# Dropping an empty lane step before the first use of rows that were fetched ahead, and slowing the first lane's pace

## The chip, the cores and the metric

The kernel runs on one core of one Trainium2 chip. The metric is the device time of one execution in microseconds. "The profile" is one execution recorded by the hardware profiler; its views group instructions by engine: PE (TensorE matmuls; PEld are its weight loads), DVE (VectorE), ACT (ScalarE), POOL (GpSimd) and SP (SyncE, which issues nearly all DMAs here). L206 is line 206 of the kernel before.

## The reference

One layer of a hybrid encoder over 1280 rows (a sample of 1024, a prompt of 256) of width 2048. After an RMSNorm one large projection gives the inputs of three groups: a bidirectional state-space scan (SSD), windowed grouped-query attention, and cross-attention to a memory of 256 rows. Their gated outputs are concatenated and projected back.

```python
hn = rms_norm(x, norm_g)
proj = hn @ w_in
xbc, z_ssd, dt_raw, q, k, v, z_att, mq, z_mem = split_cols(proj, IN_SIZES)
...                                        # conv, SSD forward and backward, gate, norm -> o_ssd
q = rms_norm(q.reshape(b, T, ATT_HEADS, ATT_HEAD_DIM), q_norm_g)
k = rms_norm(k.reshape(b, T, ATT_KV_HEADS, ATT_HEAD_DIM), k_norm_g)
o_att = window_attention(q, k, v, sink) * jax.nn.silu(z_att)
...
mq = rms_norm(mq.reshape(b, T, MEM_HEADS, MEM_HEAD_DIM), mq_norm_g)
sm = jnp.einsum('bthd,bmhd->bhtm', mq, mk) * (MEM_HEAD_DIM ** -0.5)
o_mem = jnp.einsum('bhtm,bmhd->bthd', jax.nn.softmax(sm, axis=-1), mv) * jax.nn.silu(z_mem)
return x + jnp.concatenate([o_ssd, o_att, o_mem], axis=-1) @ w_out
```

## The kernel before

**Blocks.** The rows are ten tiles of 128, in two groups of five: tiles 0 to 4 and 5 to 9. The projections run as blocks of weights. A block of 512 columns for five tiles (`block_tok`) takes 16 weight slices, k = 0 to 15, with 15 matmuls each; a feature block (`block_feat`, x0 to x5, za, zm) has 16 k of 12 matmuls. Every float32 weight slice is loaded by SP, copied on ACT into a high part (L206) and its remainder formed on DVE (L207), so that three fast matmuls stand for one exact one. There are three buffers of high and low parts (`WB`) and four raw ones (`RB`). Blocks in order: the memory's two, q of the first group, fourteen units for the first group that save products by sums (`block_pair`), kv and z1 of the first group; then for the second group x0 to x5, kv, q, za0, za1, z0, z1, mq, zm0, zm1; the output blocks o0 to o3 of the first group; and eight `block_pair` units for the output of the second.

**Lanes.** All other work is written as Python generators, one per tile, that are queued on two lanes. One lane step runs a generator from one `yield` to the next and so puts that work between block matmuls. After each k, `run` calls `pump(rates)`: each lane is owed `rates[i]` more steps, and the two take turns while either is owed at least one. A step's instructions are tied behind the weight split of that k. The last call of a generator, after its last `yield`, is a step too. `RATES` gives the pace of either lane, by group and block; feature blocks use half of it per k. `need(fn, ts)` steps a lane at once until the named tiles are done: for the keys and attention before kv of the second group, and for the outputs before they are loaded as rows for the output blocks.

- The first lane holds: small vectors, the memory's keys (`mk_prep`) and values, then `k_prep` (norm, split and transpose of the keys of a tile), `attn` (window attention) and `mem_attn` (memory attention), in the order k_prep 0-4, attn 0-3, mem_attn 0-4, k_prep 5-9, attn 4, attn 5-9, mem_attn 5-7, the second memory's keys and values, mem_attn 8-9.
- The second lane holds the scan: `dt_prep`, `ssd_up` (forward) and `ssd_down` (backward).

**Rows fetched ahead.** `k_prep`, `attn` and `mem_attn` begin with rows that an earlier block stored to DRAM. Near its end each of them calls `fetch_next()`, which issues the load for the tile behind it in the lane, if that tile is one of these three and queued by then (`fetched`). The tile itself takes the loaded rows in `taken(...)`, or issues the load there if it was not fetched. Then came a `yield` in every case, and in the next step the first use: a square on ACT (L517 in k_prep, L632 in attn, L749 in mem_attn), a sum on DVE and a power on POOL. In mem_attn of the first group, PE's transpose of the rows (`turned`, L744) comes before the square; in the second group it is a step later. L757 and L759 split the turned rows in mem_attn.

**What is behind it.** In attn: five steps on, the transposes on PE (`pq`, L653); later four scores (`psc`, L671, L672, with the clamp and maximum `nm` on DVE, L673), four times turning the weights (`ppt`, L693, copied by L694 on ACT to `pT`), and two products with the values (`po`, L703). In k_prep three steps on: the transposes (`pk`, L536) of `kh` (L528, L530). In mem_attn: scores `pms` (L772 to L774), softmax `mpr`, turns `pmt` (L794), products `pmo` (L809). Of the second lane the text names `so` (L1040, ACT's copy of the turned result), `pyb` (L1091, the backward scan's product with the state) and `pd` (L1074, transposes).

Of the kernel before, what the change touches and what calls it, by code (L numbers as in the profile page):

```python
# [28 lines left out]
CH, WB, RB, WA, WBB = 4, 3, 4, 5, 4  # L29
RBB = 4  # L30

RATES = ({'kv': (4.0, 1.0), 'z1': (2.2, 1.7)},
         {'kv': (1.5, 1.5), 'x': (2.1, 2.15), 'q': (2.25, 2.5), 'za': (2.15, 2.5), 'z0': (2.1, 2.5),
          'z1': (2.1, 2.55), 'mq': (2.0, 2.7), 'zm': (1.75, 2.75), 'o': (2.15, 2.4)})
FAR = 1e30

UNITS = (0, 8, 1, 9, 2, 10, 3, 11, 4, 12, 5, 13, 6, 7)
# [7 lines left out]
def hymba_encoder_kernel(  # L45
# [37 lines left out]
    def psum(name):  # L83
        return mix.tile([P, 512], F32, tag="mix", name=name)
# [37 lines left out]
    def rsqrt(dst, src, scale, n):  # L122
        G.tensor_scalar(out=dst, in0=src, scalar1=scale, scalar2=EPS, op0=ALU.mult, op1=ALU.add)
        G.tensor_tensor(out=dst, in0=dst, in1=mhalf[:, :n], op=ALU.pow)

    def hv(ap, n=8):
        return ap.rearrange("p (h d) -> p h d", h=n)

    def hb(ap, n, d):
        return ap.unsqueeze(2).broadcast_to([P, n, d])  # L130
# [7 lines left out]
    def queue(lane, fn, ts):  # L138
        for t in ts:
            lanes[lane].append(((fn.__name__, t), fn(t)))  # L140
# [28 lines left out]
    def need(fn, ts):  # L169

        for t in ts:
            while (fn.__name__, t) not in done:
                step(next(x for x in lanes if any(nm == (fn.__name__, t) for nm, _ in x)))
# [47 lines left out]
    def w_in_rows(name):  # L221
        return w_laid(laid_in(name), W_AT[name][1])
# [107 lines left out]
    def ev_dtkv(base):  # L330
        def f(i, ps):
            t = base + i
            r = ev.tile([P, P], F32, tag="evt" if i % 2 else "evu", name="kraw")
            A.activation(r, ps[:, 32:160], AF.Copy)
            S.dma_start(k_d[t], r)
            V.tensor_add(dt_all[:, t, :], ps[:, :32], dtb)
            V.tensor_copy(v_all[:, i + (2 if base else 0), :], ps[:, 160:288])  # L337
        return f
# [4 lines left out]
    def some_left():  # L343
        with ExitStack() as st:
            for ins in marks:
                st.enter_context(tc.issue_after(ins))
            left.popleft()()
# [67 lines left out]
    def w2(name):  # L415
        return mp.tile([P, 512], F32, tag="wa", name=name, bufs=WA)
# [64 lines left out]
    fetched = {}  # L481
# [21 lines left out]
    def taken(name, t):  # L503
        return fetched.pop((name, t)) if (name, t) in fetched else fetch[name](t)

    def fetch_next():

        name = lanes[0][1][0] if len(lanes[0]) > 1 else ("", 0)
        if name[0] in fetch:
            fetched[name] = fetch[name[0]](name[1])  # L510

    def k_prep(t):
        r = taken("k_prep", t)
        yield
        ss = sm.tile([P, 2], F32, tag="s2", name="kss", bufs=4)
        sq = w2("ksq")[:, :P]
        A.activation(sq, r, AF.Square)  # L517
        V.reduce_sum(out=ss, in_=hv(sq, 2), axis=AX.X)
        rr = sm.tile([P, 2], F32, tag="s2", name="krr", bufs=4)
        rsqrt(rr, ss, 1.0 / 64, 2)  # L520
        yield
        r3 = hv(r, 2)
        V.tensor_mul(r3, r3, hb(rr, 2, 64))
        V.tensor_mul(r3, r3, gq.unsqueeze(1).broadcast_to([P, 2, 64]))

        kh = mp.tile([P, 4, 2, 64], F32R, tag="wa", name="kh", bufs=WA)
        for d in range(2):
            A.activation(kh[:, 0:2, d, :], r3, AF.Copy)  # L528
        for d in range(2):
            V.tensor_sub(kh[:, 2:4, d, :], r3, kh[:, 0:2, 0, :].bitcast(F32))  # L530
        yield
        yield
        ps = psum("pk")
        kf = kh.rearrange("p a b d -> p (a b d)")
        for a in range(4):
            T.transpose(ps[:, a * P:(a + 1) * P].bitcast(F32R), kf[:, a * P:(a + 1) * P], identr)  # L536
        sl = t if t < 5 else t - 3
        c = slice(sl * P, (sl + 1) * P)
        V.tensor_copy(kT[:, :, c], hv(ps[:, :256], 2))
        A.activation(kL[:, :, c], hv(ps[:, 256:], 2), AF.Copy)  # L540
        fetch_next()
        yield
# [77 lines left out]
    def attn(t):  # L620
# [5 lines left out]
        s0 = k0 if t < 4 else k0 - 3  # L626
        grp, ti = divmod(t, 5)
        tc_ = slice(ti * P, (ti + 1) * P)
        q = taken("attn", t)
        yield  # L630
        sq = w2("sq")
        A.activation(sq, q, AF.Square)  # L632
        ss = sm.tile([P, 8], F32, tag="s8", name="qss", bufs=4)
# [10 lines left out]
        for b in range(2):  # L644
# [9 lines left out]
            o = mp.tile([P, 512], F32R, tag="qT", name="qT", bufs=2)  # L654
# [79 lines left out]
    def mem_attn(t):  # L734
        grp, ti = divmod(t, 5)
        tc_ = slice(ti * P, (ti + 1) * P)
        qr = taken("mem_attn", t)
        q = qr.bitcast(F32)
        yield

        def turned():
            ps = psum("pmq")
# [689 lines left out]
    def run(gen, rates, after=None, hold=0, lag=2, extra=None):  # L1432

        for k in gen:
            if after is not None:
                pend.extend(after(k))
            if hold:
                for _ in range(2 if k < KT - 4 else 0):
                    if pend:
                        u = pend.popleft()()  # L1440
                        next(u)
                        next(u)
            else:

                if loaded and (len(loaded) == lag or not pend or k >= KT - 4):
                    next(loaded.popleft())
                if pend and k < KT - 4:
                    loaded.append(pend.popleft()())
                    next(loaded[-1])

            if k >= hold:
                pump(rates)
            if extra is not None:
                extra(k)
# [101 lines left out]
    def tok(name, w, evac, after=None, grp=0):  # L1556
        run(block_tok(w, 5, evac), RATES[grp][name], after)

    def feat(name, b, evac, grp, after=None, extra=None):
        run(block_feat(f"{name}{b}", evac), [r / 2 for r in RATES[grp][name]], after, lag=3, extra=extra)  # L1560

# [7 lines left out]
    for u, unit in enumerate(units):  # L1569
# [42 lines left out]
    w_kv = w_in_rows("kv")  # L1612
    run(block_tok(w_kv, 5, ev_dtkv(0), before_last=lambda _: need(vectors, [0])), RATES[0]["kv"], hold=5,
        extra=lambda k: some_left() if left else None)
# [4 lines left out]
    def when_done(n, then):  # L1619
# [9 lines left out]
        return f  # L1629

    queue(0, mem_attn, range(5))
    run(block_tok(w_in_rows("z1"), 5, ev_gate(1, 0)), RATES[0]["z1"], refill_x(1),
        extra=when_done(1, lambda: queue(1, ssd_up, range(4))))
# [7 lines left out]
    def gate(name, c, after=None):  # L1641
        for b in range(2):
            feat(name, b, ev_gateT(c, 1, 2 * b), 1, after if b else None)

    need(attn, range(4))
    kv_shift()
    run(block_tok(w_kv, 5, ev_dtkv(5)), RATES[1]["kv"], extra=lambda k: some_left() if left else None)
    queue(0, k_prep, range(5, 10))
    queue(0, attn, [4])
    queue(1, dt_prep, [5])  # L1650
    run(block_tok(w_in_rows("q"), 5, ev_raw(q_d, 5)), RATES[1]["q"], extra=when_done(2, lambda: queue(1, ssd_up, range(4, 8))))
    gate("za", 0)
# [108 lines left out]
```

## Time and profile before

| | us |
|---|---|
| median of 3 runs | 1785.77 (1785.28 to 1787.44) |
| the profiled execution | 1785.96 |
| its span | 1784.2 |
| PE busy | 1774.6 |
| weight loads of PE busy | 1606.3 |
| DVE / ACT / POOL busy | 1245.8 / 921.5 / 547.3 |

Busy time is the union of an engine's records. A group's row gives line, engine, operation, out<-in, shapes and count, then busy time and mean ns, then the idle time of the engine just before and what ended it. A row of waits reads: who, for whom, total us, times, the longest. A row of the timeline gives start, duration, engine, line and tiles, and in brackets the idle time before it and its releaser. A row of a stretch gives its bounds, its length and the busy time of PE, PEld, DVE, ACT and POOL, then the granted clock of PE, the DMA share and GB/s. Matmuls are pipelined and their ends are modelled.

### The profile page before, as it was taken

The page shows a single profiled execution, that of the slowest core. Times are in us where ns is not written, and L with a number is a line of the kernel's source. Part 1 is how long each engine was busy: PE and PEld are TensorE (multiplying, and loading weights), DVE is VectorE, ACT ScalarE, POOL GpSimd, SP SyncE. Part 2 cuts the span into 40 slices and gives each one's busy share as a digit, 9 for nine tenths or more (in the row PEclk, how much of TensorE's full clock was granted, in tenths as well). Part 3 has the DMA queues.
Part 4 walks back from the last instruction along what each step waited for, and adds up shares of the span by engine and source line. Part 5 has one row for each costly group of instructions (what it writes and reads, how often), then busy time and mean ns, then how long its engine had stood idle before and what let it go on. Part 6 is the DMA issues. An engine that isn't in the chain of part 4 may idle for free.

```text
span 1784.2 us, 31407 instructions
## 1 busy us (share of the span) xinstructions
PE 1774.6 (99%) x10838; PEld 1606.3 (90%) x10838; DVE 1245.8 (70%) x2358; ACT 921.5 (52%) x2049; POOL 547.3 (31%) x900
## 2 busy tenths in 40 slices
PE   9999999999999999999999999999999999999999
PEld 7889999999998999999889977877988888899999
DVE  5596788888768887777665666557777644766665
ACT  5555455555434766756464565544447533533333
POOL 0105789999810100001001010000100000057775
PEclk9999999999999999999999999999999999999999
DMA  8654454445446644453635645557777764744442
GB/s 299 191 183 125 135 154 148 141 146 159 126 144 205 199 134 139 135 162 110 189 118 175 193 148 160 168 158 249 229 229 242 247 189 140 224 147 142 148 142 78
DMA packets 208207, 301.12 MB, mean 169 GB/s; under 512 B 19568, under 2 KB 86192, under 8 KB 208048
## 3 DMA queue, kind: packets, MB, share of 16 engines
q1 hardware_dynamic: 207904, 299.06, 54.5%
q8 instruction: 85, 1.39, 0.3%
q14 instruction: 74, 0.61, 0.1%
q10 hardware_dynamic: 144, 0.06, 0.0%
HBM read 236.36 MB, written 62.69 MB: 168 GB/s over the span
## 4 chain that ended last, share of the span: by engine, by line
PE 82%; issue 6%; DVE 4%; DMA 4%; POOL 2%; ACT 1%; SPq 0%; POOLq 0%; ACTq 0%; DVEq 0%
PE acc L258 9%; PE acc L260 8%; PE acc L259 8%; PE acc L1268 7%; PE acc L1270 7%; PE acc L1269 7%; PE acc L293 5%; PE acc L295 5%; PE acc L294 5%; PE accm L1268 3%; PE accm L1269 3%; PE accm L1270 3%; PE po L703 1%; PE ppt L693 1%; PE py L970 1%
## 5 line engine op out<-in xcount | busy, mean ns | idle before, releaser
L207 DVE TENSOR_TENSOR wl<-wraw,wh 128x512 fp32r<-128x512 f32 (+1 forms) x480 | 346.2, 723 | 244.0 <-ACT wh L206 238.5
L206 ACT ACTIVATE wh<-wraw 128x512 fp32r<-128x512 f32 (+1 forms) x480 | 292.2, 613 | 312.4 <-PE acc L260 147.8
L258 PE MATMUL acc<-wh,xH 128*128 128x512 f32 (+1 forms) x1088 | 418.9, 385 | 0.4 <-DVE v_all L337 0.4
L260 PE MATMUL acc<-wh,xL 128*128 128x512 f32 (+1 forms) x1088 | 410.1, 377 | 0.0
L259 PE MATMUL acc<-wl,xH 128*128 128x512 f32 (+1 forms) x1088 | 409.7, 377 | 0.0
L258 PEld LDWEIGHTS acc<-wh,xH 128*128 128x128 f32 x1088 | 204.5, 188 | 37.8 <-issue 3.4
L260 PEld LDWEIGHTS acc<-wh,xL 128*128 128x128 f32 x1088 | 204.4, 188 | 37.0 <-issue 0.2
L259 PEld LDWEIGHTS acc<-wl,xH 128*128 128x128 f32 x1088 | 204.7, 188 | 35.9 <-issue 1.6
L293 PE MATMUL acc<-xH,wh 128*128 128x320 f32 x640 | 202.8, 317 | 0.0
L294 PE MATMUL acc<-xL,wh 128*128 128x320 f32 x640 | 198.8, 311 | 0.0
L295 PE MATMUL acc<-xH,wl 128*128 128x320 f32 x640 | 198.0, 309 | 0.0
L206 ACT ACTIVATE sh<-ws 128x384 fp32r<-128x384 f32 x176 | 91.3, 523 | 204.8 <-POOL ws L1236 102.5
L207 DVE TENSOR_TENSOR sl<-ws,sh 128x384 fp32r<-128x384 f32 x176 | 123.8, 706 | 94.6 <-ACT sh L206 94.4
L1236 POOL TENSOR_TENSOR ws<-wraw 128x128 f32<-128x128 f32 x176 | 110.8, 630 | 205.8 <-DMA wraw<-in_w_in_pairs_dram 80.9
L665 POOL COPY lg<-nsink 128x2 f32<-128x2 f32 x40 | 13.6, 340 | 379.1 <-PE ppt L693 221.3
L1236 POOL TENSOR_TENSOR ws<-wraw,ws 128x128 f32<-128x128 f32 x176 | 118.7, 674 | 13.8
L293 PEld LDWEIGHTS acc<-xH,wh 128*128 128x128 f32 x640 | 120.2, 188 | 2.8 <-issue 2.2
L294 PEld LDWEIGHTS acc<-xL,wh 128*128 128x128 f32 x640 | 120.3, 188 | 1.7 <-issue 1.4
L295 PEld LDWEIGHTS acc<-xH,wl 128*128 128x128 f32 x640 | 120.2, 188 | 0.6 <-issue 0.5
L1236 POOL TENSOR_TENSOR wraw<-wraw 128x128 f32<-128x128 f32 x176 | 112.9, 642 | 13.7
L1236 POOL TENSOR_TENSOR ws<-ws,wraw 128x128 f32<-128x128 f32 x176 | 115.6, 657 | 0.0
L362 DVE SCALAR_TENSOR_TENSOR c<-u,vec,c 128x638 f32<-128x638 f32 (+1 forms) x96 | 90.0, 938 | 9.9 <-ACT c L357 9.5
(437 smaller groups left out, 3942.7 us busy)
## 6 DMA issues: line engine op xcount, KB each, us to landing
wraw<-in_w_in_laid_dram SPq DMA_DIRECT2D x176, 256.0 KB, 3.0
wraw<-in_w_in_pairs_dram SPq DMA_DIRECT2D x112, 256.0 KB, 2.7
wraw<-in_w_out_laid_dram SPq DMA_DIRECT2D x64, 256.0 KB, 3.5
wraw<-in_w_out_pairs_dram SPq DMA_DIRECT2D x64, 256.0 KB, 2.8
rf<-ac SPq DMA_DIRECT2D x40, 256.0 KB, 4.1
rb<-ac SPq DMA_DIRECT2D x40, 256.0 KB, 4.7
wraw<-in_w_mem_laid_dram SPq DMA_DIRECT2D x32, 256.0 KB, 4.4
xst<-in_x_sample_dram SPq DMA_DIRECT2D x20, 256.0 KB, 5.9
```

The source lines that it names most:

```text
L206: a = A.activation(h, raw, AF.Copy)
L207: b = V.tensor_sub(l, raw, h.bitcast(F32))
L258: T.matmul(ps[t][:, :n], sh, h[:, :n], start=(k_ == 0), stop=False)
L259: T.matmul(ps[t][:, :n], sh, l[:, :n], start=False, stop=False)
L260: T.matmul(ps[t][:, :n], sl, h[:, :n], start=False, stop=(k_ == KT - 1))
L293: T.matmul(o, sh, cur["H", q][:, m, c], start=(k == 0), stop=False)
L294: T.matmul(o, sh, cur["L", q][:, m, c], start=False, stop=False)
L295: T.matmul(o, sl, cur["H", q][:, m, c], start=False, stop=(k == KT - 1))
L1236: G.tensor_tensor(out=o, in0=x, in1=y, op=op)
L1268: T.matmul(ps[p], h, xh, start=(k_ == 0), stop=False)
L1269: T.matmul(ps[p], h, xl, start=False, stop=False)
L1270: T.matmul(ps[p], l, xh, start=False, stop=(k_ == 7))
```

## The change

In `k_prep`, `attn` and `mem_attn` the first `yield` is left out when the tile's rows were fetched ahead; the first use then comes in the tile's first step. The first lane's numbers in `RATES` are lowered for z1 of the first group and for x, q, za, z0, z1, mq, zm and o of the second; kv stays as it was in both, and the second lane's numbers stay.

```diff
-RATES = ({'kv': (4.0, 1.0), 'z1': (2.2, 1.7)},
-         {'kv': (1.5, 1.5), 'x': (2.1, 2.15), 'q': (2.25, 2.5), 'za': (2.15, 2.5), 'z0': (2.1, 2.5),
-          'z1': (2.1, 2.55), 'mq': (2.0, 2.7), 'zm': (1.75, 2.75), 'o': (2.15, 2.4)})
+RATES = ({'kv': (4.0, 1.0), 'z1': (2.1, 1.7)},
+         {'kv': (1.5, 1.5), 'x': (1.95, 2.15), 'q': (2.1, 2.5), 'za': (1.95, 2.5), 'z0': (1.9, 2.5), 'z1': (1.9, 2.55), 'mq': (1.85, 2.7), 'zm': (1.6, 2.75), 'o': (2.05, 2.4)})
...
     def k_prep(t):
+        early_ = ("k_prep", t) in fetched
         r = taken("k_prep", t)
-        yield
+        if not early_:
+            yield
...
+        early_ = ("attn", t) in fetched
         q = taken("attn", t)
-        yield
+        if not early_:
+            yield
...
+        early_ = ("mem_attn", t) in fetched
         qr = taken("mem_attn", t)
         q = qr.bitcast(F32)
-        yield
+        if not early_:
+            yield
```

## The prediction

> **What bounds the kernel now.** I read the page first, then the PE waits and the engines' busy time over the stretch in which the lanes run, then the waits of ACT on loads, and last the timeline of SP, ACT and PE around single tiles.
>
> ```profile
> span 1784.2 us, 31407 instructions
> PE 1774.6 (99%) x10838; PEld 1606.3 (90%) x10838; DVE 1245.8 (70%) x2358; ACT 921.5 (52%) x2049; POOL 547.3 (31%) x900
> ```
>
> PE is idle for 1784.2 - 1774.6 = 9.6 us in all. The change touches only what the lanes issue, so the stretch that counts goes from the first lane work behind block kv (494 us) to the last before the final stage (1562 us). Its row (PE, PEld, DVE, ACT, POOL busy; then granted clock) and the waits of PE in it:
>
> ```profile
> 494.00:1562.00 1068.00, 1064.19 (x6409) 926.26 (x6408) 730.48 (x1569) 582.11 (x1402) 87.01 (x162) 1.00 0.58 179
> ```
> ```profile
> PE pmt L794 <- DVE mpr L786: 1.4, 2, 1.3
> PE pyb L1091 <- ACT so L1040: 0.6, 1, 0.6
> PE pd L1074 <- DVE nm L673: 0.5, 1, 0.5
> PE acc L258 <- DVE v_all L337: 0.4, 1, 0.4
> PE pk L536 <- DVE kh L530: 0.3, 1, 0.3
> PE psc L671 <- ACT pT L694: 0.2, 1, 0.2
> PE psc L671 <- ACT qT L655: 0.2, 1, 0.2
> ```
>
> The stretch holds 1068.0 - 1064.2 = 3.8 us of idle PE, and the named waits add to 3.6 us. The granted clock is 1.00. What a better order of the lanes can give back is therefore a few microseconds, while what a worse order can cost has no such limit. One reservation: a matmul's record is longer than the distance to the next one.
>
> ```profile
> 700.10 0.31 PE L293 MATMUL acc<-xH,wh 128*128 128x320 f32 x1
> 700.25 0.31 PE L294 MATMUL acc<-xL,wh 128*128 128x320 f32 x1
> 700.39 0.31 PE L295 MATMUL acc<-xH,wl 128*128 128x320 f32 x1
> ```
>
> Starts are 0.15 us apart and records 0.31 us long, so gaps under about 0.16 us are covered by the record before and are in neither figure.
>
> **The change part by part.** The removed lane step is empty: with the rows already fetched, the step before the first `yield` only looks the tile up. No instruction, DMA or wait is added or taken away on any engine or queue; 31407 instructions should stay. What changes is the order in which lane work lies between block matmuls, and that follows from the paces (lane steps per k).
>
> A tile takes as many steps as it has yields, and one more for its end: k_prep 6, attn 21, mem_attn 13; one less when fetched ahead. Fetched ahead are 26 of the 30 tiles: not k_prep 0 and 5 and not mem_attn 5 and 8, since what stands before these in the lane fetches nothing or they are queued later. To turn paces into time I need the time of a k. Stretches from the count of block matmuls (16 k per block):
>
> ```profile
> 528.50:589.50 61.00, 60.64 (x289) 50.17 (x289) 53.51 (x116) 30.87 (x72) 5.28 (x8) 1.00 0.68 201
> 589.50:818.90 229.40, 228.87 (x1614) 214.47 (x1613) 174.98 (x392) 144.32 (x357) 18.86 (x31) 1.00 0.47 144
> 818.90:865.90 47.00, 45.74 (x364) 44.03 (x362) 37.77 (x85) 33.48 (x90) 5.47 (x5) 1.00 0.57 164
> 939.00:1007.30 68.30, 68.24 (x485) 66.00 (x484) 45.02 (x98) 36.20 (x95) 8.91 (x15) 1.00 0.55 173
> 1007.30:1237.40 230.10, 230.10 (x1237) 183.36 (x1235) 138.79 (x321) 125.61 (x310) 18.54 (x39) 1.00 0.56 175
> 1323.20:1466.80 143.60, 143.39 (x782) 119.91 (x781) 88.10 (x175) 78.47 (x188) 6.47 (x11) 1.00 0.74 231
> ```
>
> These are z1 of the first group (16 k, 3.81 us each), x0 to x5 (96 k, 2.39), kv of the second group (16 k, 2.94), za (32 k, 2.13), z0 to mq (48 k, 4.79) and o0, o1 (32 k, 4.49). Counting steps by the pump's rule with both sets of paces, the tiles end at the same k or one k apart (attn 3 at k 11 of x5 in both, mem_attn 4 at k 15 of q in both, attn 9 at k 9 and at k 10 of zm1, mem_attn 9 at k 1 of o2 in both); only k_prep 5 to 9 end 2 to 4 k earlier. No `need` of a first-lane tile has steps left to force in either count, so no burst of lane steps appears or goes. The second lane keeps its paces.
>
> **(1) A shorter way from load to first use.** The fetch of attn and mem_attn lies 4 steps ahead of the first use, then 3; that of k_prep 3, then 2. In z0: 4 / 2.1 = 1.90 k becomes 3 / 1.9 = 1.58 k, 0.33 x 4.79 = 1.6 us less. In x (paces halved): 3.81 k to 3.08 k, 1.7 us less. k_prep in z1: 3 / 2.2 to 2 / 2.1, 0.41 x 3.81 = 1.6 us less; in za 1.6; mem_attn in o: 4 / 2.15 to 3 / 2.05, 1.8 us less. So ACT reaches the square some 1.7 us sooner against the load. Does the load have that time? What ACT waits for these loads today, and how long a load of q takes:
>
> ```profile
> ACT ksq L517 <- DMA kr<-k: 7.2, 4, 3.7
> ACT sq L632 <- DMA q<-q: 3.9, 2, 2.2
> ACT sq L749 <- DMA mq<-mq: 3.6, 2, 2.3
> ACT mqh L757 <- DMA mq<-mT: 3.4, 3, 1.8
> ```
> ```profile
> DMA to landing us min/median/max: 2.5/3.4/4.8
> ```
>
> 11 waits, 18.1 us. Issue on SP, use on ACT and what stands behind it, for two tiles of attn, and the first and the last of the fetched-ahead tiles with little slack:
>
> ```profile
> 557.70 0.38 SPq L485 DMA_DIRECT2D kr<-k  x1
> 1136.46 0.42 SPq L490 DMA_DIRECT2D q<-q  x1
> 1237.62 0.42 SPq L490 DMA_DIRECT2D q<-q  x1
> 1440.96 0.42 SPq L498 DMA_DIRECT2D mq<-mq  x1
> ```
> ```profile
> 562.94 0.31 ACT L517 ACTIVATE ksq<-kr 128x128 f32<-128x128 f32 x1 [0.45 <-ACT wh L206]
> 1140.29 0.63 ACT L632 ACTIVATE sq<-q 128x512 f32<-128x512 f32 x1 [1.69 <-DMA q<-q]
> 1241.23 0.63 ACT L632 ACTIVATE sq<-q 128x512 f32<-128x512 f32 x1 [2.19 <-DMA q<-q]
> 1241.77 0.58 ACT L1040 ACTIVATE so<-pr 128x512 f32<-128x512 f32 x1
> 1444.03 0.61 ACT L749 ACTIVATE sq<-mq 128x512 f32<-128x512 f32 x1
> ```
> ```profile
> 1242.40 1.12 PE L1091 MATMUL pyb<-state,cc 128*128 128x512 f32 x2 [0.59 <-ACT so L1040]
> ```
>
> The tiles fall in two kinds. In 18 of the 26 the first use follows the landing by less than 1.7 us (often by 0.02: ACT stood waiting); the slack that these have adds to about 4.5 us. So ACT will wait some 18 x 1.7 - 4.5 = 26 us more, an estimate. What does PE pay? ACT is 52% busy, and most of its waiting in front of the weight split is for PE:
>
> ```profile
> ACT wh L206 <- PE acc L260: 147.8, 79, 5.7
> ```
>
> So the splits run ahead of PE until a buffer comes free, and a wait of 1 to 2 us on ACT is mostly cover used up. Of the 18.1 us that ACT waits today, 0.6 us reached PE (the row of 1242.40, where the copy `so` stood behind the square of attn 9): 3.3%. 26 x 3.3% = 0.9 us. Ends: 0, and the share of that one tile, 0.59 / 2.19 = 27%, which gives 7.0 us. I take +0.9, since ten of the eleven waits left no trace on PE. By the Trainium skill (DMA: Bandwidth & Descriptors, Anatomy of one DMA) a transfer costs a fixed 2.0 us plus its bytes over 436 GB/s, which is 2.6 us for these 256 KB; by that estimate the loads would land inside the shorter distance and this term would be nothing. The trace has a median of 3.4 us here and up to 4.8, so the row decides and the term stays.
>
> **(2) k_prep's transposes.** Fetch to transpose was 6 steps and is 5: 2.73 k to 2.38 k in z1, 1.3 us less, for the three tiles there whose chain is full (1 to 3). One of them already holds PE for 0.3 us (pk on kh). Between square and transpose there are still 3 steps, at a slower pace, 0.25 us more. Where the landing sets the chain it loses 1.3, where the engines' queues set it it gains 0.25; I take half the loss for the one tile that waits, +0.6. Ends: -0.3 and 3 x 1.3 = +3.9.
>
> **(3) mem_attn of the first group transposes straight from the load on PE,** in the step that moves. The closest is mem_attn 1, in kv, where the pace stays 1.5:
>
> ```profile
> 833.68 4.01 DMA mq<-mT
> ```
> ```profile
> 839.86 0.45 PE L744 MATMUL pmq<-identr,mq 128*128 128x128 f32 x4
> ```
>
> It lands at 837.69 and is used 2.2 us later; one step in kv is 2.94 / 1.5 = 2.0 us. That leaves 0.2 us: cost 0, ends 0 and 2.0.
>
> **(4) The slower pace.** A step in z0 lasts 4.79 / 1.9 = 2.52 us instead of 2.28: 0.24 us more for each chain from one step to the next. Of the waits of PE above, pd (0.5), and psc twice (0.2 each) lie in first-lane steps with a slower pace, and 0.5 of these 0.9 us goes. The 1.4 of pmt lies in kv, whose pace is unchanged, and stays; 0.6 (pyb) is of part 1. So -0.5. Ends: 0 and all the named waits, -3.6.
>
> **Sum** against the profiled execution's own 1785.96 us (1784.2 of span and 1.8 around it): +0.9 + 0.6 + 0 - 0.5 = +1.0, 1787.0. The median of the runs shown is 1785.77, 0.2 lower, so the forecast is **1786.8 us**. About 0.2% (3.6 us) is what a measurement of this kernel can tell from no change, so I call it no change.
>
> **The rivals.** *A: load waits on ACT reach PE.* ACT works in order; behind the square stand copies that empty PE's accumulators and the next weight split. If the new waits pass on at the share of attn 9, the cost is 7.0 us instead of 0.9: 1785.8 + 7.0 + 0.6 - 0.5 = 1792.9. For it: attn 5, 6, 7 and 9 and mem_attn 6 and 7 all start at the landing already. Against: ten waits without effect. It decides from a share of 3.6 / 26 = 14%. *B: the spacing is worth more.* If all the named waits go and loads cost nothing, 1785.8 - 3.6 = 1782.2; to be clearly faster it also needs gaps hidden under the overlapping records, and with as much again it gives 1778.6. Against: the sum of named waits is just the bound, and 2.4 of its 3.6 us lie where the pace does not slow (pmt and v_all in kv) or where the load wait is the cause (pyb). Beside this, the Trainium skill (Perfetto Trace Analysis, Identifying the Most-Contended Engine) says that matmul busy time is a bad measure of headroom and weight-load busy time a better one; by the row of the stretch that would be 1068.0 - 926.3 = 142 us not loading. The 0.15 us starts show the narrow blocks packed, so it moves the chance little. *C: the change does not do what it says:* a fetched load whose buffer comes free late would make the shorter distance void. The fetch itself is not moved, and what it waits for is unchanged; the time is then that of the sum without part 1, 1785.9, within the same band.
>
> **How the numbers follow.** Sum and C, within 0.2% (1782.2 to 1789.3): 0.56. A: 0.31, as it needs only a seventh of the new waits to pass on. B: 0.13. The range for 8 in 10 reaches into both: low 1781, short of B's hidden gaps; high 1794, A with a little of part 3. For the likeliest alone, 1784 to 1789.
>
> **What would show it.** The count of instructions unchanged; ACT's four rows of waits on these loads up from 18 to about 44 us in total; PE's named waits in the stretch still under 6 us; the wait of psc and pd shorter; pmt's 1.3 us still there. If PE's waits on `so`, on weight splits or on kh grow past 4 us, A holds; if idle PE in the stretch falls under 1 us, B. The forecast is wrong too if the new order puts two lanes' PE work into one k, for which the rows of before have no price.

## The result, and the profile after

| | before | after |
|---|---|---|
| median, us | 1786.32 (1785.28 to 1787.85, 8 runs) | 1791.76 (1788.96 to 1797.96, 8 runs) |
| the profiled execution, us | 1785.96 | 1790.47 |
| its span, us | 1784.2 | 1788.8 |
| idle PE, 494 to 1566.6 us | 3.8 | 8.5 |

The ratio over the executions is 1.0034, with an interval of 1.0018 to 1.005: the change makes the kernel slower by about a third of a percent. The forecast was "no change", 1786.8 us. The time lies inside its range of 1781 to 1794 us, on the slower side, but outside the 1782.2 to 1789.3 us that it called no change.

First the head of the page of after and its row for the stretch in which the lanes run. Lines of after are one lower than before near the weight split (L205, L206, L257 to L259) and up to five higher in mem_attn and the scan.

```profile
span 1788.8 us, 31420 instructions
PE 1774.5 (99%) x10838; PEld 1605.0 (90%) x10838; DVE 1249.9 (70%) x2358; ACT 921.8 (52%) x2049; POOL 549.7 (31%) x900
```
```profile
494.00:1566.60 1072.60, 1064.08 (x6402) 924.71 (x6402) 733.00 (x1567) 581.70 (x1400) 88.04 (x161) 1.00 0.57 178
```

The engines issue as many operations as before (10838, 2358, 2049 and 900; the 13 more instructions are none of these), and PE is busy just as long, 1774.5 against 1774.6 us. What grew is PE's idle time between 494 and 1566.6 us: 1072.6 - 1064.1 = 8.5 us instead of 3.8. These 4.7 us are the 4.6 by which the span grew. So the question is for what PE stands. Its waits in this stretch of after, from the view of waits (total us, times, the longest):

```profile
PE pmq L749 <- DMA mq<-mT: 1.9, 1, 1.9
PE pst L901 <- ACT fh L915: 1.6, 1, 1.6
PE pyb L1096 <- ACT so L1045: 1.3, 1, 1.3
PE pxs L894 <- DMA xc<-xbc_d: 1.2, 1, 1.2
PE pxs L894 <- DVE xs L896: 0.7, 1, 0.7
PE pmt L799 <- DVE mpr L791: 0.4, 2, 0.3
...
PE psc L674 <- DVE nm L676: 0.2, 1, 0.2
PE psc L674 <- ACT pT L697: 0.2, 1, 0.2
```

The rows of before hold no wait of PE for `pst`, `pxs` or `pmq`. `pyb` grew from 0.6 to 1.3; `pmt` shrank from 1.4 to 0.4; `pd` (0.5) and `pk` (0.3) are gone. New or grown are 1.9 + 1.6 + 0.7 + 1.2 + 0.7 = 6.1 us, gone are 1.8. Of the 6.1, 4.2 (`pst`, `pyb`, `pxs`) stand in front of work of the second lane, the scan, which the change does not touch.

ACT's waits on the loads that are fetched ahead:

```profile
ACT sq L635 <- DMA q<-q: 10.3, 5, 3.4
ACT ksq L518 <- DMA kr<-k: 6.5, 4, 2.2
ACT mqh L762 <- DMA mq<-mT: 5.7, 3, 4.1
ACT sq L754 <- DMA mq<-mq: 2.8, 2, 1.7
```

Together 25.3 us, against 18.1 before. They rose by 7, not by the 26 of the forecast.

Each large new wait, followed back one step. First `pst`, in the timelines of ACT and of PE in after:

```profile
1345.29 1.65 ACT L199 ACTIVATE xH<-chd,vec 128x640 fp32r<-128x640 f32 x2 [1.89 <-DMA chd<-oT]
1346.84 0.62 ACT L205 ACTIVATE wh<-wraw 128x512 fp32r<-128x512 f32 x1
1347.37 1.53 ACT L199 ACTIVATE xH<-chd,vec 128x640 fp32r<-128x640 f32 x2
1348.80 1.26 ACT L958 ACTIVATE rf<-rf,wj_all 128x128 f32<-128x128 f32 x4
1349.97 0.61 ACT L915 ACTIVATE fh<-xf 128x512 fp32r<-128x512 f32 x1
```
```profile
1350.64 0.50 PE L901 MATMUL pst<-fh,bth 128*128 128x512 f32 x1 [1.65 <-ACT fh L915]
```

ACT stood for 1.89 us on the rows of an output block (`chd`), and four rows of ACT later PE stood 1.65 us for `fh`, which comes behind them in ACT's order. None of the loads that are fetched ahead is in this chain. The order is not new either: before, SP issues these four loads between the same neighbours, ACT has the same five rows, and PE has `pst` at the same place. What differs is how long the four loads took, in before (the first line) and in after:

```profile
DMA to landing us min/median/max: 4.3/5.1/5.6
DMA to landing us min/median/max: 6.2/6.8/7.3
```

Next `pxs` on SP's queue and on PE:

```profile
1088.46 8.14 SPq L212 DMA_DIRECT2D wraw<-in_w_in_laid_dram  x2
1096.69 0.56 SPq L734 DMA_DIRECT2D oT<-oT  x1
1097.34 1.07 SPq L980 DMA_DIRECT2D yd<-yo  x2
1098.46 1.57 SPq L850 DMA_DIRECT2D xc<-xbc_d  x2
```
```profile
1105.26 0.51 PE L894 MATMUL pxs<-identr,xc 128*128 128x128 f32 x4 [1.22 <-DMA xc<-xbc_d]
```

SP was held for 8.1 us on two weight loads, then came the store of the first lane (`oT`) and one of the second (`yd`), and only then the scan's own load. In the trace of before the same load is issued at 1094.0, 4.4 us sooner and ahead of the store of `oT`, and nothing waits for it. The other wait of `pxs`, 0.7 us at 639.9, is for a copy on DVE (`xs`) that comes behind a weight's remainder (`wl`) in after and ahead of it in before. `pyb`, at 1245.7, has its old neighbours on ACT and PE; its load is issued 1.7 us ahead of the transposes `pr` on PE that come just before, and was 2.5 us ahead in before. Last `pmq`, SP's issue and PE's use for mem_attn 2, in before (the first pair) and in after (the second):

```profile
857.40 0.52 SPq L496 DMA_DIRECT2D mq<-mT  x1
...
865.51 0.54 PE L744 MATMUL pmq<-identr,mq 128*128 128x128 f32 x4
```
```profile
854.59 0.54 SPq L495 DMA_DIRECT2D mq<-mT  x1
...
860.16 0.51 PE L749 MATMUL pmq<-identr,mq 128*128 128x128 f32 x4 [1.86 <-DMA mq<-mT]
```

Before, PE came to this tile 8.1 us after the issue; after, it wanted it 860.16 - 1.86 - 854.59 = 3.7 us behind the issue. The way shrank by 4.4 us, not by the 2.0 that one step takes on average in kv.

The runs of after spread over 9 us, those of before over 2.6. The four executions of after whose granted clock was 1.00 took 1789.0 to 1790.5 us; the four at 0.998 or 0.999 took 1793.1 to 1798.0. At full clock the loss is thus 1789.8 - 1786.3 = 3.4 us by the middle executions, less than the 5.4 us of the medians; the rest is in the executions at a lower clock. What lowers the clock is told in the last section.

### The profile page after: what moved, and what is told of

Same layout as the page of the kernel before. It is cut to its first block, busy times and chain, and to the rows that moved or that the text cites. A ratio compares the mean times of both kernels' runs of the same rounds, so it can differ in the third digit from the quotient of the medians.

```text
span 1788.8 us, 31420 instructions
## 1 busy us (share of the span) xinstructions
PE 1774.5 (99%) x10838; PEld 1605.0 (90%) x10838; DVE 1249.9 (70%) x2358; ACT 921.8 (52%) x2049; POOL 549.7 (31%) x900
## 4 chain that ended last, share of the span: by engine, by line
PE 86%; issue 6%; DMA 3%; DVE 3%; POOL 1%; ACT 1%; SPq 0%; POOLq 0%; ACTq 0%; DVEq 0%
PE acc L257 10%; PE acc L259 10%; PE acc L258 10%; PE acc L1273 7%; PE acc L1275 7%; PE acc L1274 7%; PE acc L292 5%; PE acc L294 5%; PE acc L293 5%; PE accm L1273 3%; PE accm L1274 3%; PE accm L1275 3%; PE po L706 1%; PE ppt L696 1%; PE py L975 1%
## 5 line engine op out<-in xcount | busy, mean ns | idle before, releaser
L206 DVE TENSOR_TENSOR wl<-wraw,wh 128x512 fp32r<-128x512 f32 (+1 forms) x480 | 347.6, 726 | 235.6 <-ACT wh L205 226.2
L205 ACT ACTIVATE wh<-wraw 128x512 fp32r<-128x512 f32 (+1 forms) x480 | 292.3, 613 | 293.3 <-PE acc L259 143.0
L257 PE MATMUL acc<-wh,xH 128*128 128x512 f32 (+1 forms) x1088 | 417.5, 384 | 0.4 <-DVE v_all L336 0.4
L259 PE MATMUL acc<-wh,xL 128*128 128x512 f32 (+1 forms) x1088 | 410.1, 377 | 0.0
L257 PEld LDWEIGHTS acc<-wh,xH 128*128 128x128 f32 x1088 | 204.3, 188 | 37.5 <-issue 3.3
L259 PEld LDWEIGHTS acc<-wh,xL 128*128 128x128 f32 x1088 | 204.2, 188 | 36.9 <-issue 0.2
L205 ACT ACTIVATE sh<-ws 128x384 fp32r<-128x384 f32 x176 | 91.3, 523 | 203.9 <-POOL ws L1241 101.8
L206 DVE TENSOR_TENSOR sl<-ws,sh 128x384 fp32r<-128x384 f32 x176 | 122.6, 699 | 92.8 <-ACT sh L205 90.8
```

The lines of the kernel that those rows point to most:

```text
L205: a = A.activation(h, raw, AF.Copy)
L206: b = V.tensor_sub(l, raw, h.bitcast(F32))
L257: T.matmul(ps[t][:, :n], sh, h[:, :n], start=(k_ == 0), stop=False)
L259: T.matmul(ps[t][:, :n], sl, h[:, :n], start=False, stop=(k_ == KT - 1))
```

## The experiments

Three theories stand behind the expectations. **L**: the shorter way from load to first use costs. **R**: any shift of the first lane's steps against the block matmuls costs (or gains), because its steps then meet the second lane's at other places on the queues of ACT, DVE, SP and PE. **S**: the slower pace as such costs. All ratios are against the kernel before, run on the same chip beside it.

| run | what it is | ratio | interval | idle PE in the stretch, us | ACT's load waits, us |
|---|---|---|---|---|---|
| before | | 1 | | 3.8 | 18.1 |
| after | | 1.0034 | 1.0018 to 1.005 | 8.5 | 25.3 |
| fetch_early | after, fetch one step sooner | 1.0025 | 1.0016 to 1.0034 | 6.2 | 16.2 |
| mem0_keep | after, step kept in mem_attn 0 to 4 | 1.0025 | 1.0015 to 1.0035 | 6.7 | 20.1 |
| attn_moved | after, attn drops a later step | 1.0041 | 1.0029 to 1.0053 | 8.3 | 21.0 |
| paces_98 | before, first lane's paces x 0.98 | 1.0031 | 1.0019 to 1.0043 | 7.4 | 29.5 |
| fetch_late | before, fetch one step later | 1.0004 | 0.9995 to 1.0013 | 4.2 | 17.5 |
| phase_half | before, half a lane step ahead | 1.0039 | 1.0025 to 1.0052 | 7.0 | 15.0 |
| paces_102 | before, first lane's paces x 1.02 | 1.0008 | 0.9999 to 1.0016 | 3.5 | 18.6 |
| before_fetch_early | before, fetch one step sooner | 1.0005 | 0.9996 to 1.0013 | 5.3 | 8.6 |
| use_early | before, use a step sooner, step count kept | 1.0001 | 0.9993 to 1.001 | 3.8 | 16.7 |
| after_phase | after, half a lane step ahead | 1.0008 | 0.9999 to 1.0017 | 3.2 | 12.7 |
| steps_only | the step dropped, paces of before | 1.0017 | 1.0008 to 1.0026 | 6.2 | 18.4 |
| paces_only | paces of after, step kept | 1.0012 | 1.0003 to 1.002 | 5.4 | 18.5 |

The idle time is the length less PE's busy time of the window 494 to 1566.6 us in each profile. The ratio goes with it, roughly, and not with ACT's waits: the six kernels of the study with least idle PE (3.2 to 5.3 us) are the six with the lowest ratios (up to 1.0008), while phase_half is among the slowest with fewer load waits than before. Three of the profiles also hold stretches at half clock, which are not idle time and come on top: two in attn_moved, one in phase_half and one in paces_only.

**fetch_early.** In k_prep, attn and mem_attn of after:

```diff
+        fetch_next()
...
         yield
-        fetch_next()
```

> The changed kernel with each fetch issued one lane step earlier (attn beside its last turn, mem_attn beside its second turn, k_prep a step before its transposes), so that load and first use are as many steps apart as before the change; paces and tile ends are those of the changed kernel. Theory L (the way from load to first use has become too short, and PE pays for loads that have not landed): the wait of pmq on its load (1.9 us) and most of pyb on so (1.3 us) go, idle PE in the lane stretch falls from 8.5 us to about 4, the time to 1786 to 1788 us. Theory R (any shift of the first lane's steps against the block's k costs some microseconds, whichever step it is): no better than the changed kernel, 1790 to 1793 us, with other waits.

1789.98 us, 1.0025. The order on PE is that of after; seven of mem_attn's ten loads and that of k_prep 5 are issued 13 to 30 us sooner, those of attn are not. The wait of `pmq` is gone and idle PE fell from 8.5 to 6.2 us, but `pyb` on `so` (1.6), `pst` on `bl` (0.9) and on `fh` (0.8) and `pxs` (1.4 in two rows) stand. So L holds for the one tile, some 1.9 us, and for no more: 6.2 is still 2.4 above before. The interval overlaps that of after, so the gain is read from the profile, not from the times.

**mem0_keep.** The step stays in mem_attn of the first group, and the pace of q is raised for it:

```diff
-         {'kv': (1.5, 1.5), 'x': (1.95, 2.15), 'q': (2.1, 2.5), 'za': (1.95, 2.5), 'z0': (1.9, 2.5), 'z1': (1.9, 2.55), 'mq': (1.85, 2.7), 'zm': (1.6, 2.75), 'o': (2.05, 2.4)})
+         {'kv': (1.5, 1.5), 'x': (1.95, 2.15), 'q': (2.35, 2.5), 'za': (1.95, 2.5), 'z0': (1.9, 2.5), 'z1': (1.9, 2.55), 'mq': (1.85, 2.7), 'zm': (1.6, 2.75), 'o': (2.05, 2.4)})
...
-        if not early_:
+        if not early_ or t < 5:
             yield
```

> The changed kernel, but mem_attn of the first group (tiles 0 to 4) keeps its step between load and first use; q's pace is raised to 2.35 so that these tiles end where they did. Theory L: PE's wait of pmq on the load of mq (1.9 us in the changed kernel's profile) is gone; 1789.5 to 1790 us, and the spread between executions, which comes from how long such a load takes, shrinks. Theory R: no better than 1791 us.

1790.17 us, 1.0025. From its waits of PE:

```profile
PE pd L1079 <- DMA ydT<-yd: 2.2, 1, 2.2
PE pr L1043 <- ACT pT L697: 1.4, 1, 1.4
PE pyb L1096 <- DVE oT L709: 0.8, 1, 0.8
```

`pmq` no longer waits here either, and its 1.9 us are replaced by waits that neither before nor after has. Mending one place by moving steps made three new ones at other places.

**attn_moved.** The first `yield` of attn stays, and one of three empty ones behind the square goes. The way from load to square is then that of before:

```diff
-        if not early_:
-            yield
+        yield
...
-        for _ in range(3):
+        for _ in range(2 if early_ else 3):
             yield
```

> The changed kernel, but in a fetched-ahead attn the step between load and square stays, and one of the three steps between square and product goes in its place: as many steps, the same paces and tile ends, the load distance of before. Theory L: ACT's waits of the square on the load of q fall by 5 us or more, pyb's wait on so falls from 1.3 us to 0.6 or less; 1789.5 to 1791 us. Theory R: 1791 us or more.

1794.34 us, 1.0041. ACT's waits for q fell from 10.3 to 7.3 us, and the time did not: idle PE is 8.3 us, in nearly the places of after (`pmq` 1.9, `pxs` 2.6, `pyf` on `qT` 1.0, `pyb` 0.9), and PE's order is nearly that of after. So taking 3 us of waits for attn's loads, the core of rival A, off ACT gained nothing. It is a weak test: the square changed its place in ACT's order in only four of the ten tiles, and L had asked for 5 us. This profile also has two stretches at half clock, of which the last section tells.

**paces_98.** Nothing but the first lane's paces (kv as before) is changed, to 0.98 of before:

```diff
-RATES = ({'kv': (4.0, 1.0), 'z1': (2.2, 1.7)},
-         {'kv': (1.5, 1.5), 'x': (2.1, 2.15), 'q': (2.25, 2.5), 'za': (2.15, 2.5), 'z0': (2.1, 2.5),
-          'z1': (2.1, 2.55), 'mq': (2.0, 2.7), 'zm': (1.75, 2.75), 'o': (2.15, 2.4)})
+RATES = ({'kv': (4.0, 1.0), 'z1': (2.156, 1.7)},
+         {'kv': (1.5, 1.5), 'x': (2.058, 2.15), 'q': (2.205, 2.5), 'za': (2.107, 2.5), 'z0': (2.058, 2.5),
+          'z1': (2.058, 2.55), 'mq': (1.96, 2.7), 'zm': (1.715, 2.75), 'o': (2.107, 2.4)})
```

> The kernel before, with all steps kept and the first lane's paces 2% lower in the blocks that the change touches; no tile's steps have to be forced by a need. Theory L: the distance between load and use grows by 2%, so nothing is lost: 1785 to 1787 us. Theory R: the order against the k's shifts in every block, 1789 to 1792 us.

1791.52 us, 1.0031, with every step kept. ACT's load waits are the longest of all here (29.5 us), but none of PE's larger waits is for a load or for a copy of the loaded rows. PE waits for `pmt` 2.0 (four times), `pst` 1.3 and 0.9, `ppt` 1.1 and 0.9 us. A shift of two percent costs as much as the whole change: R, or S.

**fetch_late.** In before, `fetch_next()` goes behind the `yield` that follows it, in all three tiles.

```diff
-        fetch_next()
         yield
+        fetch_next()
```

> The kernel before with its paces and all its lane steps, but each fetch issued one lane step later (attn and mem_attn with their last product, k_prep in its closing step): load and first use are as far apart in steps as in the changed kernel, and no work on PE, ACT or DVE moves against the k's. Theory L (the shorter way from load to use is what costs): 1789 to 1792 us, with PE waits on the load of mq or on copies behind a square. Theory R (the shift of the first lane's steps is what costs): 1786 to 1788 us; the small part that L has by the earlier runs, some 1.5 us at most.

1787.39 us, 1.0004. The order on every engine came out as before's (two single instructions of DVE apart), so moving the fetch by one step did not change where the load stands on SP. The run says nothing on L. It shows instead what the same order gives when it is measured again: 1.0004 with 0.9995 to 1.0013, and 4.2 us of idle PE instead of 3.8. Single waits differ by more than that sum. Here PE waits for `fh` at the place where after has its 1.65 us and before nothing:

```profile
1345.78 0.51 PE L896 MATMUL pst<-fh,bth 128*128 128x512 f32 x1 [0.79 <-ACT fh L910]
```

The four loads of `chd` ahead of it took up to 6.2 us, between the 5.6 of before and the 7.3 of after. A wait of under a microsecond in one profile is therefore no proof of a changed order.

**phase_half.** Before, with half a step more owed to the first lane ahead of z1 of the first group. Paces, steps and the steps between load and use are those of before:

```diff
+    owed[0] += 0.5
     run(block_tok(w_in_rows("z1"), 5, ev_gate(1, 0)), RATES[0]["z1"], refill_x(1),
```

> The kernel before with paces, steps and load distances unchanged, but the first lane starts the block z1 of the first group with half a step in hand, so that until block zm1 each of its steps comes half a step earlier against the k's. Theory L: no loss, 1786 to 1787 us. Theory R: 1789 to 1792 us, with PE waits on second-lane chains (pxs, pst, pyb) that the kernel before does not have.

1794.48 us, 1.0039; the one of its five executions at full clock took 1791.8. This decides against S, and against L as the main cause: ACT waits for the loads 15.0 us, 3 less than before, and the loss is as large as that of after. Its largest wait, in the timelines of ACT and PE:

```profile
1070.13 1.27 ACT L953 ACTIVATE rf<-rf,wj_all 128x128 f32<-128x128 f32 x4
1071.31 1.26 ACT L953 ACTIVATE rb<-rb,wj_all 128x128 f32<-128x128 f32 x4
1072.47 0.61 ACT L206 ACTIVATE wh<-wraw 128x512 fp32r<-128x512 f32 x1
1072.99 0.58 ACT L655 ACTIVATE qT<-pq 128x512 fp32r<-128x512 f32 x1
```
```profile
1073.62 0.44 PE L671 MATMUL psc<-kT,qT 128*128 128x384 f32 x1 [2.02 <-ACT qT L655]
```

This is a meeting of the lanes as rows show it. The first lane's second copy `qT` stands on ACT behind 2.5 us of the second lane's work (`rf`, `rb`) and a weight split, and PE, whose next instruction is the score that needs it, stands for 2.02 us. ACT does nothing that it would not do anyway, and is about half busy over the stretch.

**paces_102.** As paces_98, with factor 1.02:

```diff
-RATES = ({'kv': (4.0, 1.0), 'z1': (2.2, 1.7)},
...
+RATES = ({'kv': (4.0, 1.0), 'z1': (2.244, 1.7)},
+         {'kv': (1.5, 1.5), 'x': (2.142, 2.15), 'q': (2.295, 2.5), 'za': (2.193, 2.5), 'z0': (2.142, 2.5),
+          'z1': (2.142, 2.55), 'mq': (2.04, 2.7), 'zm': (1.785, 2.75), 'o': (2.193, 2.4)})
```

> The kernel before with the first lane's paces 2% higher in the blocks that the change touches. Theory R (any shift costs): 1789 to 1792 us as with 2% lower. Theory S (a lower pace as such costs, since the first lane comes later): 1785 to 1787 us.

1788.21 us, 1.0008, idle PE 3.5 us. So not every shift costs 3 us or more, as R in its plain form had it; this one cost a microsecond or two, or nothing that can be told from fetch_late. R is to be read as "a shift draws a new set of meetings", some cheap and some dear.

**before_fetch_early.** The edit of fetch_early, in before.

```diff
+        fetch_next()
...
         yield
-        fetch_next()
```

> The kernel before with its paces and steps, and each fetch issued one lane step earlier. No work on PE, ACT or DVE moves against the k's. Theory L: ACT's waits on these loads (18.1 us) fall to under 8 us, pyb's wait on so (0.6 us) goes, and the time is 0.5 to 1.5 us better: 1785 to 1786 us. Theory R: within 0.5 us of the kernel before.

1787.21 us, 1.0005. PE's order is before's, seven of mem_attn's ten loads and that of k_prep 5 are issued 15 to 25 us sooner, and ACT's waits fall to 8.6 us. Nothing is gained by it: ten microseconds fewer of load waits on ACT, and 5.3 us of idle PE against 3.8. So the ten microseconds of waits that went had cost before nothing that can be measured. Attn's loads did not move, and `pyb` still waits on `so` (0.9).

**use_early.** Before with its paces and its count of steps; where the tile was fetched ahead, the first use goes into the first step and an empty step follows it, so that everything later stays in place:

```diff
+        early_ = ("k_prep", t) in fetched
...
-        yield
+        if not early_:
+            yield
...
+        if early_:
+            yield
```

with the same in mem_attn, and in attn a fourth empty step behind the square instead of a third.

> The kernel before with its paces and its number of steps, but in a fetched-ahead tile the first use (the square, its sum and the power; in mem_attn of the first group also the transposes on PE) goes into the first step, and the empty step follows it. The way from load to first use is a step shorter, as in the changed kernel, and nothing else moves: the order of PE's matmuls and transposes differs only by those transposes. Theory L: 1789 to 1792 us. Theory R (the meeting of the lanes' steps is what costs, not the load): 1786 to 1788 us, the most part of it a wait of pmq on mq of up to 2 us.

1786.84 us, 1.0001. Idle PE is 3.8 us as before, and ACT waits 16.7 us, not more. The row of its stretch:

```profile
494.00:1566.60 1072.60, 1068.81 (x6433) 930.35 (x6432) 731.64 (x1571) 583.82 (x1405) 86.45 (x163) 1.00 0.58 179
```

But the edit reached the engines only in part. By the order of the traces the first use moved in nine tiles: the square in k_prep 1, 2, 3 and 9 and attn 8, and the transposes on PE with the square behind them in mem_attn 1 to 4. In the other tiles that are fetched ahead the square stands behind the same instruction on ACT as in before. For attn 9, whose rows of before stand in the prediction, SP's issue and ACT's square here:

```profile
1237.26 0.42 SPq L490 DMA_DIRECT2D q<-q  x1
1240.91 0.64 ACT L638 ACTIVATE sq<-q 128x512 f32<-128x512 f32 x1 [1.98 <-DMA q<-q]
```

It is 3.6 us from the issue to the square in both, and ACT waits 1.98 us where it waited 2.19. So a step that is moved in a generator moves an instruction on its engine's queue only sometimes. What fixes the order when the kernel is built was not followed. The run shows that L is worth nothing in the nine tiles, mem_attn 2 among them, where the transposes came 6.1 us behind the issue instead of 8.1 and did not wait; on the others it says nothing.

**after_phase.** The half step of phase_half, in after:

```diff
+    owed[0] += 0.5
     run(block_tok(w_in_rows("z1"), 5, ev_gate(1, 0)), RATES[0]["z1"], refill_x(1),
```

> The changed kernel, with half a step in hand for the first lane at the start of z1 of the first group, as phase_half was to the kernel before. Theory R: other steps meet, so the waits of the changed kernel (pxs on xc, pst on fh, pyb on so) are replaced by others, and the time is somewhere between 1786 and 1795 us, not tied to 1791.8. Theory L: the load distance is the same, so 1791 to 1793 us with pmq's wait on mq still there.

1788.52 us, 1.0008. From its stretch and PE's waits:

```profile
494.00:1566.60 1072.60, 1069.36 (x6432) 930.04 (x6431) 734.76 (x1571) 583.50 (x1403) 91.57 (x162) 1.00 0.58 179
```
```profile
PE pmt L799 <- DVE mpr L791: 1.4, 2, 1.2
PE pxs L894 <- DVE xs L896: 0.6, 1, 0.6
```

Idle PE is 3.2 us, less than before's. The waits of `pmq`, of `pxs` on its load and of `pyb` are gone, `pst` is down to 0.3, and the 1.4 us of `pmt` are back. The same half step that costs before 0.39% takes most of the loss from after. At full clock, ten of the eleven executions, the middle is 1788.1 us, 1.7 above before's 1786.4, so the 3.4 us of after are halved; the rest of the gain is that executions at a lower clock are rare. The loss is therefore not in dropping the step nor in the lower paces as such, but in the order and the spacing that came out of them.

**steps_only** and **paces_only.** The two halves of the change, each alone. steps_only is after with the numbers of before:

```diff
-RATES = ({'kv': (4.0, 1.0), 'z1': (2.1, 1.7)},
...
+RATES = ({'kv': (4.0, 1.0), 'z1': (2.2, 1.7)},
+         {'kv': (1.5, 1.5), 'x': (2.1, 2.15), 'q': (2.25, 2.5), 'za': (2.15, 2.5), 'z0': (2.1, 2.5),
+          'z1': (2.1, 2.55), 'mq': (2.0, 2.7), 'zm': (1.75, 2.75), 'o': (2.15, 2.4)})
```

and paces_only is before with the numbers of after:

```diff
-RATES = ({'kv': (4.0, 1.0), 'z1': (2.2, 1.7)},
...
+RATES = ({'kv': (4.0, 1.0), 'z1': (2.1, 1.7)},
+         {'kv': (1.5, 1.5), 'x': (1.95, 2.15), 'q': (2.1, 2.5), 'za': (1.95, 2.5), 'z0': (1.9, 2.5), 'z1': (1.9, 2.55), 'mq': (1.85, 2.7), 'zm': (1.6, 2.75), 'o': (2.05, 2.4)})
```

> The step dropped as in the change, with the paces of before: the first lane runs ahead and its tiles end up to 8 k earlier. Theory R: another order, another set of waits, 1787 to 1794 us. Theory L: as the changed kernel or a little worse, since the pace is faster and the way from load to use shorter still: 1792 to 1794 us.

> The paces of the change with all steps kept: the first lane falls behind, by the counts up to 9 k, and four steps of attn 3 are forced at once before kv of the second group, three more than before at the last flush. Theory R: 1789 to 1796 us, with waits at the forced steps. Theory L: load distances are longer than before, so only the forced steps cost: 1787 to 1789 us.

steps_only: 1789.74 us, 1.0017; PE waits for `pst` 1.3, `pmq` 1.1, `pd` 0.9, `pk` 0.9 us. paces_only: 1788.9 us, 1.0012; `ppt` 1.6 and 0.9, `py` 1.0 us. Either half costs something, and at places that after itself mostly does not have (`ppt`, `py` and `pk` don't wait there, and `pst` is the only large one that steps_only and after share). That 0.17% and 0.12% nearly add to 0.34% is not a sum of two causes, since the waits are others; at full clock the middles lie 3.3 and 1.5 us above before's and do not add to the 3.4 of after. No kernel of the study beat the one before.

## Why the prediction was right in its range and wrong in its mechanism

**What bounds the kernel** held. The loss is idle PE in the stretch, and small losses add there without anything to hide them: 4.7 us of idle time made 4.6 us of span.

**(1) The way from load to use, +0.9, of 0 to 7.0.** The place that it named came true at its size: `pyb` on `so` behind the square of attn 9 grew from 0.59 to 1.29 us, +0.7. But it came from 7 us of new waits on ACT and not 26. The 26 took every square to reach ACT 1.7 us sooner against its load. In after ACT comes to the first use 3.7 us behind the issue, on average over the 26 tiles, instead of 4.6: 0.9 us sooner. use_early shows a reason: the order on the engines is not simply that of the steps, and most squares kept their place there. (The tiles fetched ahead are 27: in before_fetch_early the load of k_prep 5 came at 920.2 instead of 941.5 us when `fetch_next()` moved, so mem_attn 4 fetches it. This changes little. The 2.6 us for a load in the prediction come from a fit for transfers that GpSimd issues; SP issues these, and those of q took 2.5 to 4.8 us.)

**(2) The transposes of k_prep, +0.6.** The sign was wrong: the 0.3 of `pk` is gone, which was the lower end.

**(3) The transposes straight from the load, 0, of 0 to 2.0.** The upper end came true: 1.9 us, and for mem_attn 2, not for mem_attn 1, which had been called the closest. The first mistake is the average. A step was taken as 2.94 / 1.5 = 2.0 us; but steps run only at the end of a k, one or two of them, so a tile's use moves by about a whole k or more, or stays. For mem_attn 1 the way from issue to use fell from 6.2 to 5.7 us, for mem_attn 2 from 8.1 to 3.7. The second is the load, which took up to 5.4 us instead of 4.0:

```profile
DMA to landing us min/median/max: 5.0/5.2/5.4
```

(the landing times of the two loads in after, 830 to 866 us). In use_early, where mem_attn 2 had 6.1 us and a load of 4.0, there is no wait. fetch_early shows this term nearly by itself: with the wait of 1.9 gone idle PE falls by 2.3 us.

**(4) The slower pace, -0.5.** `pd`'s 0.5 is gone, as said, while two waits of `psc` of 0.2 each remain, so the size is right by one row. But `pmt`, which was to stay since kv keeps its pace, fell from 1.4 to 0.4: a step in kv had moved against the k's although its pace had not.

**The step that failed** is the one ahead of the sum: since tiles end "at the same k or one k apart" and "the second lane keeps its paces", the order was treated as unchanged but for the steps' spacing, and its cost as nothing. By the rows of after, the terms of the forecast come to +0.7 - 0.3 + 1.9 - 0.5 - 1.0 (`pmt`) = +0.8, close to the +1.0 that was forecast. That is chance: of the four only the pace came out as it was worked out. The other 3.9 us are `pst` 1.6, `pxs` 1.2 and 0.7 and two waits of 0.2, none of which is in the sum. The two of `pxs` are hand-overs of the scan to PE that stand behind other work on SP and DVE than before. `pst` stands where it stood and waits for a load that took longer, and fetch_late, in before's own order, has half of this wait; whether the new order made that load slower is open. PE's waits on the view of after add to 8.3 us, where the forecast had set under 6 as its sign. Its last sentence named what would make it wrong ("two lanes' PE work into one k, for which the rows of before have no price"), and its opening said that a worse order has no such limit; neither was given a chance. paces_98 and phase_half put the price at 0.3 to 0.4%, paces_102 and after_phase at under 0.1%. That the range held is luck too: its upper part was there for rival A and part 3, and the loss came for the most part from neither.

**The rivals.** A's 1792.9 us lies near the measured 1791.76, but not its mechanism: its sign was more than 4 us on `so`, the weight splits and `kh`, and these grew by 0.4 together; phase_half, with its loss and fewer load waits than before, also speaks against it. B, the gain from spacing, did not come: what left (1.8 us) was less than what came (6.1). C was half right: the edit does not do all that it says, though not because a buffer comes free late but because most squares keep their place on ACT. It took the rest to be nothing as well.

**What stays open.** No row of a profile told beforehand which order is dear. Before, paces_102, use_early and after_phase have 3.2 to 3.8 us of idle PE, fetch_late and before_fetch_early 4.2 and 5.3, the eight others, after among them, 5.4 to 8.5, and why one half step helps the one and hurts the other is known only afterwards, meeting by meeting.

## What to carry to other kernels

Where two streams of small work are threaded between matmuls that fill PE, a step that does nothing is still a place in the order: removing it, or changing a pace by two percent, draws a new set of meetings on the engines' queues, and with under 4 us of idle time left there is more to lose than to gain. Price such a change by the spread over a few neutral shifts (half a step, two percent of pace), not by the average distance between steps, and look at the other lane's hand-overs to PE first. Read from the trace whether the order on the queues moved at all before a null result is believed: one moved step left all of it in fetch_late, and most squares in use_early, where they were. To test whether the loss belongs to the change, shift the changed kernel by half a step.

## What the runs showed of the hardware

A wait of PE well below 3.4 us can be followed by 3.41 us at half clock. Windows of attn_moved (length, then PE, PEld, DVE, ACT and POOL busy, granted clock, DMA share, GB/s):

```profile
860.40:863.78 3.38, 1.56 (x13) 1.59 (x14) 1.01 (x2) 1.68 (x4) 0.00 (x0) 1.00 0.89 284
863.78:867.20 3.42, 3.42 (x16) 3.42 (x15) 1.95 (x8) 0.68 (x3) 1.20 (x2) 0.50 0.37 120
1106.13:1109.54 3.41, 1.69 (x13) 1.31 (x11) 1.11 (x3) 0.63 (x1) 0.00 (x0) 1.00 1.07 276
1109.54:1112.95 3.41, 3.20 (x10) 2.65 (x11) 3.33 (x9) 1.02 (x2) 0.00 (x0) 0.50 1.03 323
```

and PE's timeline at the first of them:

```profile
862.22 0.51 PE L748 MATMUL pmq<-identr,mq 128*128 128x128 f32 x4 [1.91 <-DMA mq<-mT]
...
863.56 0.29 PE L258 MATMUL acc<-wl,xH 128*128 128x288 f32 x1
863.69 0.35 PE L259 MATMUL acc<-wh,xL 128*128 128x288 f32 x1
863.84 0.44 PE L257 MATMUL acc<-wh,xH 128*128 128x288 f32 x1
864.08 0.44 PE L258 MATMUL acc<-wl,xH 128*128 128x288 f32 x1
```

After a 3.4 us window in which PE was busy for only 1.56 us, matmuls start 0.24 us apart instead of 0.13, so the 3.42 us do the work of about 3.42 x 0.13 / 0.24 = 1.9: a single wait of 1.9 us costs about 1.5 us more. The second stretch is alike, behind 1.69 us of busy PE. phase_half has one from 1075.02 us on, behind the 2.02 us wait of `qT`, in a window with 1.40 us of busy PE, and paces_only one behind waits of 1.6 and 0.6 us. The starts of the two stretches of attn_moved are 1109.54 - 863.78 = 245.76 us apart, which is 72 times 3.413: they lie on one grid. In the profiled execution of after the same wait of 1.9 us for `pmq` is not followed by one. Its window of the grid, and the one of paces_only with the window behind it:

```profile
858.45:861.87 3.42, 1.71 (x14) 1.74 (x15) 1.16 (x2) 1.80 (x4) 0.00 (x0) 1.00 0.89 274
1333.33:1336.74 3.41, 1.26 (x7) 0.72 (x7) 1.95 (x4) 3.08 (x6) 0.19 (x1) 1.00 0.84 322
1336.74:1340.15 3.41, 3.11 (x9) 2.67 (x10) 3.41 (x11) 3.27 (x10) 0.00 (x0) 0.50 0.68 203
```

With all fourteen traces cut into windows of their grid, the changes of the clock giving its place and the ends of the span left out, the four windows with least busy PE (1.26, 1.40, 1.57 and 1.69 us; the row from 860.40 starts 0.03 us late in its window) are the four that a half-clock window follows. The next is that of after, at 1.71, half of 3.41, and all others have more than 2.0. So in these traces a window of the grid in which PE is busy for less than half of it is followed by one at half clock, and the same wait can fall into one window or be shared by two. How near to half the limit lies is finer than the modelled ends of matmuls can show. That the grid lies elsewhere in each execution would explain why the executions of after at 0.998 of the clock are the long ones; there is no trace of them, so this is argued, not shown. It also explains only a part: two such stretches make about 3 us, and these executions were 3 to 8 us longer than the middle of those at full clock, 1789.8.

The Trainium skill (TensorE: Matmul & The Clock Gate, What's actually happening) states a free-running window of 4096 cycles, 3413 ns, and the trace agrees to the third digit. Its section HAM oscillation — how this bites in real kernels gives as the rule no idle gaps of PE above about 3.4 us; here waits of 1.6 to 2.0 us were enough, so by this trace the measured waits decide and the rule is too generous.
